# Hybrid decoder block on one core: the prologue's scale sums as columns, and the first token block's work put ahead of the second's

## The chip, the cores and the metric

The kernel runs on one core of a Trainium2 chip. The time is device microseconds (us) of that core for one launch; before the change it is 2329.9 us, the median of three runs (2327.43 to 2331.16). The core has five engines that run side by side, each through its own list of instructions in order: TensorE (PE; the loading of its stationary operand is shown apart as PEld), VectorE (DVE), ScalarE (ACT), GpSimd (POOL) and SyncE (SP), which here only issues DMA transfers. They wait for one another through semaphores.

## The reference, cut to what matters

A decoder block on 2048 tokens of width 1024, with modulation by a vector c, all in float32:

```python
mod = jax.nn.silu(c) @ w_cond[l] + b_cond[l]          # w_cond: 1024 x 6144
shift_m, scale_m, gate_m, shift_f, scale_f, gate_f = [
    m[:, None, :] for m in jnp.split(mod, N_MOD, axis=-1)]

h = rmsnorm(x, g_mix_pre[l]) * (1.0 + scale_m) + shift_m
proj = h @ w_in[l]                                      # w_in: 1024 x 2048
q, k, v, u = jnp.split(proj, [SB_WIDTH, 2 * SB_WIDTH, 3 * SB_WIDTH], axis=-1)
...
x = x + gate_m * rmsnorm(mix, g_mix_post[l])
h = rmsnorm(x, g_ffn_pre[l]) * (1.0 + scale_f) + shift_f
f = (jax.nn.silu(h @ w_gate[l]) * (h @ w_up[l])) @ w_down[l]
x = x + gate_f * rmsnorm(f, g_ffn_post[l])
```

The change lies in the first lines: the sums over c that give the shift and the scale, the norm of the rows, and the first products of `h @ w_in`.

## The kernel before, in words

**Data.** The tokens form four blocks of 512 (`TB`), each of four tiles of 128 rows. The width of 1024 is eight parts of 128 (`kc` or k). `w_in` comes in chunks of 128 output columns, in the order of `chunks`: chunk 0 is q 0, chunk 1 is k 0, chunk 2 is q 1, chunk 3 is u 0, and so on. A float32 operand of a product is held as two f32r tiles, a high one (a cast by ACT, L58) and a low one (source minus high, L59, on DVE or POOL), and a product is three: L68 high by high, L69 with the low half of the tokens, L70 with the low half of the weights (`mm3`). `chunk_split` makes one quarter of a chunk's two tiles: ACT the high, POOL the low.

**Order.** The orders of PE, ACT, DVE and POOL in this phase are those in which the code is written; no scheduler moves anything. SP issues its DMAs in written order too, and a DMA that waits for its buffer holds up all behind it. Chunks' raw weights have two buffers (`w32`); the third chunk's load takes the first chunk's, so it waits for POOL's last low quarter of chunk 0.

**The sums of shift and scale.** silu(c) is `cs`, a column for each kc. The 1024 columns of the shift and those of the scale are done in two halves of 512, half 0 and half 1, and each half in four pairs of kc. `sums_load` issues a pair's two loads of 512 KB (`wcs` for the shift, `wc` for the scale); `sums_step` works on it. The shift is accumulated on DVE as `acc0` (L205 for kc 0, L207 for the others), and needs a sum over the 128 partitions at the end. The scale of half 0 is two products of 1 x 512 a pair on PE (L549, the column of `cs` stationary, the weights moving), which ends as a row. The scale of half 1 is DVE (even kc, L551), ACT (odd kc, L553) and POOL (L555) in `acc1`. `sums_end` turns all into columns: L566 sums `acc0` over the partitions with a moving operand of one column of ones, L572 turns the row into columns (half 0), L570 sums `acc1` (half 1). From these come `am` and `bm`, the multiplier and the addend of the modulation.

**Rows.** The four rows of block 0 (tiles of 128 tokens) are loaded first, squared on ACT for the norm (L297), scaled on DVE, and turned by PE: `turn_rows(j)` makes eight 128x128 transposes of row j (L529) in two banks, copied out by ACT (L533) and DVE (L535) into `turned`. `modulate0` then makes the tokens' high half on ACT (L583), `h` on DVE (L584) and the low half (L585) on POOL for even kc and DVE for odd. Block 1's rows are loaded into `early_lo`, normed, scaled in place (L301: j 0 and 2 on DVE, 1 and 3 on ACT, L301 too), and turned kc by kc (`turn1`, four transposes, L594) behind which the same three steps stand (L583 to L585).

**First products.** `first_products(n, tb, ks)` makes the three products a k for chunk n and block tb. Chunks 0 to 2 are done here for both blocks: k 0 to 3, which need half 0 alone, of block 0 and then of block 1, and then, once half 1 is there, k 4 to 7 of both. The eight banks of PSUM go by name: z0 to z2, w0 and w1 (`t_ps`), a0 and a1, mm. At each finished chunk a store of q or k (cast, low, DMA: `store_qk`) or the pooling sums of u (`pool_ops`, L366 to L388) are queued, one step of which `run_small` emits.

**The rest of the sums.** `rest_of_cond` is a chain of small steps for the parts 2 to 5 of `w_cond` (two gates, the FFN's shift and scale): each step issues one load of 512 KB and one accumulation, on DVE (L205, L207) for kc 0 to 5 and on ACT and POOL for 6 and 7; then come the adding of both (L264), and on PE the gate product `gp` (L236, L237) or the columns `cp` (L218). Six of its steps are emitted among block 1's k 4 to 7. From chunk 3 on, `weave` goes through `pieces` (one k of one chunk and block, three products, at a time), and lets a step of `rest` in every 2.9 pieces, from the first on.

Where the times need a fixed point, it is one of PE's work: 168 groups of three products done and eight turns of block 1's rows.

## Time and profile before

| | |
|---|---|
| runs | 2327.43, 2329.9, 2331.16 us (median 2329.9) |
| profiled execution | 2330.08 us, of which its span (first to last instruction) 2328.3 |
| PE busy | 2260.6 us, 97% of the span |
| PEld busy | 1854.3 us, 80% |
| DVE busy | 1629.2 us, 70% |
| POOL busy | 1317.6 us, 57% |
| ACT busy | 1163.5 us, 50% |
| DMA | 274.51 MB read, 128.45 MB written, mean 174 GB/s |
| granted TensorE clock, mean | 0.990 of full speed |

Shares are of the whole span, of which the part that the change touches is less than a tenth. Times within the span count from the first instruction. A row of the list of instructions in order of time reads: start, duration, engine, line, operation, tiles written <- read, shape, count, and in brackets the idle time ahead and what ended it. A matmul's record ends when its result is out, and records overlap; so the step from one start to the next, not the duration, is what a product takes of PE.

### The profile page before, as it was taken

What the parts mean: (1) busy time and instruction counts of PE and PEld (TensorE: products, weight loads), DVE (VectorE), ACT (ScalarE), POOL (GpSimd) and SP (SyncE); (2) the same over time, 40 slices, a digit from 0 to 9 for tenths busy, and PEclk for the clock granted to TensorE, in tenths of its full rate; (3) what the DMA queues carried; (4) which work ended last, traced back from release to release, by engine and by line L of the source; (5) the groups of instructions that cost most, each with busy time, mean ns of one, the idle gap of its engine ahead of it and who ended that gap; (6) DMA issues with size and microseconds to landing.
All of it is one profiled execution on the core that took longest, in us unless ns stands there. A gap on an engine that the chain in (4) does not pass through costs nothing.

```text
span 2328.3 us, 33054 instructions
## 1 busy us (share of the span) xinstructions
PE 2260.6 (97%) x10589; PEld 1854.3 (80%) x10589; DVE 1629.2 (70%) x2222; ACT 1163.5 (50%) x2411; POOL 1317.6 (57%) x1619
## 2 busy tenths in 40 slices
PE   6999999999999999999999999999999999999997
PEld 4778778888888777887888888888888888888885
DVE  6764549999999966756666565887766556565556
ACT  4323649899999854444323232554533323234444
POOL 4541337787778954555787878331476665641004
PEclk9999999999999999999999999999999999999998
DMA  8785764343435536655545555876754333328554
GB/s 286 257 288 193 259 210 119 99 111 91 128 105 164 161 111 195 213 193 181 171 154 163 158 159 181 272 247 214 257 172 128 99 113 91 114 91 285 189 195 145
DMA packets 307115, 405.15 MB, mean 174 GB/s; under 512 B 19254, under 2 KB 179578, under 8 KB 303868
## 3 DMA queue, kind: packets, MB, share of 16 engines
q1 hardware_dynamic: 302620, 400.68, 53.7%
q10 hardware_dynamic: 4320, 2.36, 0.4%
q8 instruction: 83, 1.36, 0.2%
q14 instruction: 92, 0.75, 0.1%
HBM read 274.51 MB, written 128.45 MB: 173 GB/s over the span
## 4 chain that ended last, share of the span: by engine, by line
PE 81%; DVE 6%; DMA 4%; POOL 4%; issue 3%; ACT 2%; SPq 0%; POOLq 0%; DVEq 0%; ACTq 0%
PE wt L828 4%; PE t_u L70 3%; PE t_u L68 3%; PE t_u L69 3%; PE t_g L69 3%; PE t_g L68 3%; PE t_g L70 3%; PE dn0p L69 3%; PE dn0p L70 3%; PE dn0p L68 3%; PE dn1p L69 3%; PE dn1p L68 3%; PE dn1p L70 3%; PE av L843 3%; PE av L844 2%
## 5 line engine op out<-in xcount | busy, mean ns | idle before, releaser
L817 POOL TENSOR_TENSOR w<-sg,pr 128x512 f32<-128x512 f32 (+2 forms) x320 | 307.3, 960 | 39.8 <-DVE pr L811 21.6
L1177 POOL TENSOR_TENSOR s<-s,cu 128x512 f32<-128x512 f32 x88 | 132.5, 1512 | 238.2 <-DVE cu L1176 145.8
L811 DVE TENSOR_TENSOR_SCAN pr<-pr,carry,begin 128x512 f32<-128x512 f32 x192 | 244.4, 1273 | 0.0
L798 ACT ACTIVATE sg<-z 128x512 f32<-128x512 f32 (+2 forms) x320 | 182.0, 569 | 49.6 <-PE z L796 35.5
L59 DVE TENSOR_TENSOR wtl<-wt,wth 128x512 fp32r<-128x512 f32 (+1 forms) x320 | 189.8, 593 | 20.5 <-ACT wth L58 19.6
L58 ACT CAST wth<-wt 128x512 fp32r<-128x512 f32 (+1 forms) x320 | 181.3, 567 | 13.0 <-PE wt L828 13.0
L800 ACT ACTIVATE pr<-z 128x512 f32<-128x512 f32 (+2 forms) x320 | 181.4, 567 | 0.0
L828 PE MATMUL wt<-ident,w 128*128 128x128 f32 x1088 | 173.9, 274 | 4.7 <-POOL w L817 2.3
L59 DVE TENSOR_TENSOR u_s_l<-u_s,u_s_h 128x512 fp32r<-128x512 f32 x66 | 65.4, 991 | 150.6 <-ACT u_s_h L58 150.6
L828 PEld LDWEIGHTS wt<-ident,w 128*128 128x128 f32 x1088 | 134.8, 141 | 35.4 <-POOL pr L808 3.2
L1167 ACT ACTIVATE s<-s 128x512 f32<-128x512 f32 x88 | 55.7, 633 | 192.0 <-DVE s L1166 192.0
L843 PE MATMUL av<-wth,vt 128*128 128x512 f32 (+1 forms) x320 | 129.9, 406 | 6.4 <-ACT o L848 6.3
L69 PE MATMUL dn0p<-w0p_l,g0p_h 128*128 128x512 f32 x308 | 121.0, 393 | 0.4 <-DVE w0p_l L59 0.4
L68 PE MATMUL dn0p<-w0p_h,g0p_h 128*128 128x512 f32 x308 | 120.6, 392 | 0.0
L70 PE MATMUL dn0p<-w0p_h,g0p_l 128*128 128x512 f32 x308 | 120.5, 391 | 0.0
L59 DVE TENSOR_TENSOR u_a_l<-u,u_a_h 128x512 fp32r<-128x512 f32 x66 | 76.2, 1156 | 62.7 <-ACT u_a_h L58 62.7
L844 PE MATMUL av<-wtl,vt 128*128 128x512 f32 (+1 forms) x320 | 118.5, 370 | 1.5 <-DVE wtl L59 1.3
L795 PE MATMUL z<-kt,qt 128*128 128x512 f32 (+2 forms) x320 | 117.6, 368 | 1.7 <-ACT pr L800 1.5
L58 ACT CAST g_s_h<-g_s 128x512 fp32r<-128x512 f32 x66 | 39.5, 620 | 157.6 <-POOL g_s L1109 80.7
L796 PE MATMUL z<-kt,qt 128*128 128x512 f32 (+2 forms) x320 | 117.1, 366 | 0.0
L69 PE MATMUL dn1p<-w1p_l,g1p_h 128*128 128x512 f32 x292 | 114.5, 392 | 0.0
L68 PE MATMUL dn1p<-w1p_h,g1p_h 128*128 128x512 f32 x292 | 114.3, 392 | 0.0
(652 smaller groups left out, 7184.5 us busy)
## 6 DMA issues: line engine op xcount, KB each, us to landing
g<-in_w_gate_dram SPq DMA_DIRECT2D x42, 512.0 KB, 5.0
u<-in_w_up_dram SPq DMA_DIRECT2D x42, 512.0 KB, 5.2
wc<-in_w_cond_dram SPq DMA_DIRECT2D x32, 512.0 KB, 5.7
qt<-qd SPq DMA_DIRECT2D x64, 256.0 KB, 3.9
wd<-in_w_down_dram SPq DMA_DIRECT2D x44, 256.0 KB, 2.9
tdt<-wd SPq DMA_DIRECT2D x44, 256.0 KB, 2.0
w0p<-tdt SPq DMA_DIRECT2D x44, 256.0 KB, 3.9
w1p<-tdt SPq DMA_DIRECT2D x44, 256.0 KB, 2.9
```

The lines of the kernel that those rows point to most:

```text
L58: nc.scalar.copy(hi, src)
L59: low.tensor_tensor(lo, src, raw(hi), ALU.subtract)
L68: nc.tensor.matmul(ps, lh, rh, start=first and i == 0, stop=False)
L69: nc.tensor.matmul(ps, lh, rl, start=False, stop=False)
L70: nc.tensor.matmul(ps, ll, rh, start=False, stop=last and i == n - 1)
L798: nc.scalar.activation(sg[:, 0:L], z[:, 0:L], AF.Sigmoid, scale=0.125)
L800: nc.scalar.activation(pr[:, 0:L], z[:, 0:L], AF.Sigmoid, scale=-0.125)
L811: nc.vector.tensor_tensor_scan(pr[:, 0:L][:, ::-1], pr[:, 0:L][:, ::-1], begin[:, TB - L:][:, ::-1], zero if carry is None else carry, ALU ...
L817: nc.gpsimd.tensor_tensor(w[:, 0:L], sg[:, 0:L], pr[:, 1:L + 1], ALU.mult)
L828: nc.tensor.transpose(wt[:, i * P:(i + 1) * P], wss[u][i][:, b * P:(b + 1) * P], ident)
L843: nc.tensor.matmul(av[:, lo0:], vb, wh[:, lo0:], start=first, stop=False)
L844: nc.tensor.matmul(av[:, lo0:], vb, wl[:, lo0:], start=False, stop=last)
```

## The change

1. **Scale sums as columns, in both halves.** A pair's scale is now eight products with a 128x128 slice of the weights as the stationary operand and the column of `cs` as the moving one, 128 x 1 each, summed into four columns of a bank (`sums[half]`). The four products that sum `acc0` for the shift go into the same bank. The row, its copy and its turn into columns are gone, and half 1's steps on DVE, ACT and POOL with `acc1` too.
2. **Turns of block 0.** Rows 0, 1 and 2 are turned ahead of the first pair's products, row 3 behind them.
3. **Order of the work.** Block 0 comes whole, chunks 0 to 2 and chunk 3 as well, ahead of block 1. Block 1's turns 0 and 1 stand among chunk 3's products, the others among its own, a pair of k ahead. Chunk 3's block 1 becomes the first piece of the weave.
4. **Loads.** Block 1's four rows are loaded behind all the sums of half 1, the fourth chunk right after, and the fifth chunk's load and splits stand in the prologue and at the start of the weave.
5. **Engines.** One low quarter of chunk 0 and one of chunk 1 go to DVE; all four rows of block 1 are scaled by DVE; their squares go into `junk` instead of a tile of their own.
6. **The rest of the sums.** Eight of its steps instead of six stand ahead of the weave, the others start one piece later, and the steps for v's weights at 96 instead of 104 (the weave has one task less).

The diff, cut to its core:

```diff
-            return lambda: nc.scalar.mul(xs, xt, r) if j % 2 else nc.vector.tensor_scalar_mul(xs, xt, r)
+            return lambda: nc.vector.tensor_scalar_mul(xs, xt, r)
...
-            if not half:
-                nc.tensor.matmul(sums[0:1, :], cs[:, kc:kc + 1], wc[:, kk], start=kc == 0, stop=kc == KC - 1)
-            elif not kk:
-                cond_step(acc1[:, 0], kc, wc[:, kk])
-            else:
-                nc.scalar.mul(wc[:, kk] if pair else acc1[:, 1], wc[:, kk], cs[:, kc:kc + 1])
-                if pair:
-                    nc.gpsimd.tensor_tensor(acc1[:, 1], acc1[:, 1], wc[:, kk], ALU.add)
+            for col in range(4):
+                nc.tensor.matmul(sums[half][:, col:col + 1], wc[:, kk, col * P:(col + 1) * P], cs[:, kc:kc + 1],
+                                 start=kc == col == 0, stop=False)
...
+        for col in range(4):
+            nc.tensor.matmul(ps[:, KC + col:KC + col + 1], acc0[:, (4 * half + col) * P:(4 * half + col + 1) * P], ones[:, 0:1],
+                             start=False, stop=col == 3)
...
-    for pair in range(4):
-        turn_rows(pair)
+    for j in range(3):
+        turn_rows(j)
+    sums_step(0, 0, *coming[0])
+    turn_rows(3)
+    for pair in range(1, 4):
         sums_step(0, pair, *coming[pair])
...
+    chunk_split(loaded[0], 1, nc.vector)
+    sums_end(0)
+    sums[1] = psum("z0", 1, "am1")
+    modulate0(0, 1)
+    first_products(0, 0, 0, 1)
+    chunk_split(loaded[1], 0, nc.vector)
+    chunk_split(loaded[0], 2)
+    modulate0(2, 3)
+    chunk_split(loaded[1], 1)
+    chunk_split(loaded[0], 3)
     loaded.append(chunk_load(chunks[2], 0, [tokp.tile([P, KC, P], F32R, tag="xs", name=f"third{n}") for n in "hl"]))
     coming += [sums_load(1, pair) for pair in range(2, 4)]
...
+    early1 = [row_load(1, j) for j in range(4)]
...
+    sums_end(1)
...
+    pairs = ((0, 1), (2, 3), (4, 5), (6, 7))
+    for ks in pairs[2:]:
         for n in range(3):
             first_products(n, 0, *ks)
+            run_small()
+    for ks in pairs:
+        first_products(3, 0, *ks)
+        if ks[0] < 4:
+            turn1(ks[0] // 2)
+    run_small()
+    for ks in pairs:
+        for n in range(3):
+            first_products(n, 1, *ks)
+            if n < 2 and ks[0] < 6:
+                turn1(ks[0] + 2 + n)
+            run_small()
             if n < 2:
...
+                next(rest)
+            if (n, ks[0]) == (0, 6):
+                loaded.append(chunk_load(chunks[4], 0))
...
     weave(pieces(0, chunks, tasks, loaded),
-          [(rest, 0, 2.9), (v_weight_ops(), 104, 1.9)])
+          [(fifth_ops(), 0, 1), (rest, 1, 2.9), (v_weight_ops(), 96, 1.9)])
```

How this moves instructions, at three places; a row is line, operation, tile written <- tiles read, shape, and how often it stands there in a row.

PE, from the first turn to the first product of chunk 0, before (`x_j_pt` are the turned parts of row j, `wc_0_p` is pair p of the scale's weights in half 0, `acc` the shift's sums):

```order
L549 MATMUL am<-wc_0_0_315,cs 1x512 x2
L529 MATMUL x_1_pt_342<-ident,early_hi 128x128 x4
L529 MATMUL x_1_pt_348<-ident,early_hi 128x128 x4
L549 MATMUL am<-wc_0_1_318,cs 1x512 x2
L529 MATMUL x_2_pt_358<-ident,early_hi 128x128 x4
L529 MATMUL x_2_pt_364<-ident,early_hi 128x128 x4
L549 MATMUL am<-wc_0_2_321,cs 1x512 x2
L529 MATMUL x_3_pt_374<-ident,early_hi 128x128 x4
L529 MATMUL x_3_pt_380<-ident,early_hi 128x128 x4
L549 MATMUL am<-wc_0_3_324,cs 1x512 x2
L566 MATMUL am_columns_424<-ones,acc_310 128x1 x4
L572 MATMUL am_columns_424<-ones,am_row 128x1 x4
```

and of the change, from the turn of row 2 on:

```order
L528 MATMUL x_2_pt_348<-ident,early_hi 128x128 x4
L528 MATMUL x_2_pt_354<-ident,early_hi 128x128 x4
L548 MATMUL am_311<-cs,wc_0_0_313 128x1 x8
L528 MATMUL x_3_pt_370<-ident,early_hi 128x128 x4
L528 MATMUL x_3_pt_376<-ident,early_hi 128x128 x4
L548 MATMUL am_311<-cs,wc_0_1_316 128x1 x8
L548 MATMUL am_311<-cs,wc_0_2_319 128x1 x8
L548 MATMUL am_311<-cs,wc_0_3_322 128x1 x8
L556 MATMUL am_311<-ones,acc_310 128x1 x4
L68 MATMUL first_0_446<-hth_270,wq_0_h 128x512
```

The 512-wide products between the turns are gone; eight one-column products stand in the place of two wide ones, and three such groups follow one another.

SP, the loads behind the first two chunks, before (`early_lo` are block 1's rows, `wcs` and `wc_1_p` the pairs of half 1, the second `wq` the third chunk, `wu` the fourth):

```order
L513 DMA early_lo<-in_x_dram 128x1024 x4
L539 DMA wcs<-in_w_cond_dram 128x2x512
L541 DMA wc_1_0_403<-in_w_cond_dram 128x2x512
...
L413 DMA wq_0_32_410<-in_w_in_dram 128x8x128
L539 DMA wcs<-in_w_cond_dram 128x2x512
L541 DMA wc_1_2_413<-in_w_cond_dram 128x2x512
L539 DMA wcs<-in_w_cond_dram 128x2x512
L541 DMA wc_1_3_416<-in_w_cond_dram 128x2x512
L413 DMA wu_0_32_669<-in_w_in_dram 128x8x128
```

and of the change:

```order
L414 DMA wq_0_32_471<-in_w_in_dram 128x8x128
L538 DMA wcs<-in_w_cond_dram 128x2x512
L540 DMA wc_1_2_474<-in_w_cond_dram 128x2x512
L538 DMA wcs<-in_w_cond_dram 128x2x512
L540 DMA wc_1_3_477<-in_w_cond_dram 128x2x512
L514 DMA early_lo<-in_x_dram 128x1024 x4
L414 DMA wu_0_32_539<-in_w_in_dram 128x8x128
```

The rows have moved from the front to behind the last pair; the third chunk's load still stands ahead of the pairs 2 and 3.

DVE, where block 1's k 4 to 7 are modulated, before (`h_k` is part k of block 1's tokens before its low half is taken off, `acc` from here on the sums of part 2, `q_0` and `k_0` stores):

```order
L584 TENSOR_SCALAR h_4_682<-x_4_677,am,bm 128x512
L584 TENSOR_SCALAR h_5_697<-x_5_692,am,bm 128x512
L585 TENSOR_TENSOR ht1b<-h_5_697,ht1b 128x512
L584 TENSOR_SCALAR h_6_718<-x_6_713,am,bm 128x512
L59 TENSOR_TENSOR q_0_722<-first_0_448,q_0_722 128x512
L584 TENSOR_SCALAR h_7_737<-x_7_732,am,bm 128x512
L585 TENSOR_TENSOR ht1b<-h_7_737,ht1b 128x512
L59 TENSOR_TENSOR k_0_741<-first_0_495,k_0_741 128x512
L59 TENSOR_TENSOR q_0_751<-first_0_553,q_0_751 128x512
L205 TENSOR_SCALAR acc_762<-wc_0_765,cs 128x1024
L258 TENSOR_TENSOR acc_762<-acc_762,br_763 1x1024
```

and of the change, from k 2 on (`us`, `um` and `uf` are the pooling sums of chunk 3's block 0):

```order
L569 TENSOR_SCALAR h_2_741<-x_2_736,am,bm 128x512
L373 TENSOR_TENSOR us_0_1_745<-u_0_725 128x527
L205 TENSOR_SCALAR acc_747<-wc_0_750,cs 128x1024
L258 TENSOR_TENSOR acc_747<-acc_747,br_748 1x1024
L569 TENSOR_SCALAR h_3_766<-x_3_761,am,bm 128x512
L570 TENSOR_TENSOR ht1a<-h_3_766,ht1a 128x512
L384 SCALAR_TENSOR_TENSOR um_0_770<-us_0_1_745,u_0_725 128x512
L387 TENSOR_TENSOR uf_772<-us_0_1_745,rcnt 128x2
L388 TENSOR_TENSOR um_0_770<-uf_772,u_0_725 128x2
L207 SCALAR_TENSOR_TENSOR acc_747<-wc_1_776,cs,acc_747 128x1024
L569 TENSOR_SCALAR h_4_797<-x_4_792,am,bm 128x512
```

Before, all of block 1's modulation stood ahead of the first sum of part 2; now these sums and the pooling stand between its parts.

More of the change, by code (lines that the diff above doesn't have):

```diff
@@ L519, in block_kernel @@
     acc0 = new_acc(0)
-    sums = z_ps("am")
-    row = cond.tile([1, TB], F32, tag="brow", bufs=1, name="am_row")
-    acc1 = cond.tile([P, 2, TB], F32, tag="acc", bufs=2, name="acc1")
+    sums = {0: z_ps("am0")}
     halves = [slice(half * TB, (half + 1) * TB) for half in range(2)]
@@ L597, in block_kernel @@
     first_ps = {}
[L598 removed]
+    first_banks = {(0, 0): mm_only, (3, 0): mm_ps, (0, 1): av_ps, (1, 1): av_ps}
     def first_products(n, tb, *ks):
@@ new lines, in block_kernel, with fifth_ops @@
+    for ks in pairs:
[9 more added lines that the diff above has]
+            run_small()
+            if n < 2:
+                next(rest)
+            if (n, ks[0]) == (0, 6):
+                loaded.append(chunk_load(chunks[4], 0))
+    def fifth_ops():
+        for part in range(4):
+            chunk_split(loaded[4], part)
+            yield
@@ L679, in block_kernel @@
+    tasks = [(n, tb) for n in range(3, len(chunks)) for tb in range(2)][1:]
     wvs = []
```

95 lines of the change are left out of this document (29 added, 66 removed).

## The prediction

> **What bounds the kernel now.** I read the page first, then stretches of the prologue, then TensorE's waits, then its instructions in order of time. The stretches:
>
> ```profile
> 0.00:82.20 82.20, 62.09 (x257) 43.61 (x258) 54.95 (x83) 37.17 (x66) 36.10 (x61) 0.92 0.77 265
> 100.00:110.00 10.00, 5.72 (x24) 3.84 (x22) 9.93 (x10) 5.41 (x9) 6.82 (x5) 0.98 0.79 281
> 160.00:200.00 40.00, 40.00 (x178) 33.13 (x177) 24.03 (x40) 13.59 (x35) 11.28 (x15) 1.00 0.65 213
> ```
>
> The columns are stretch, length, busy time of PE, PEld, DVE, ACT and POOL, granted clock, DMA share, GB/s. PE is the bound: in 160 to 200 us it is busy throughout, in the first 82 only for 62. What it loses before 170 us moves the end. After the gate product of part 5 (near 170 us) each engine's order is the same in both kernels, so the change is worth what it does to PE's time before that, one for one.
>
> ```profile
> PE am_columns L566 <- DVE acc L207: 3.7, 2, 3.1
> PE u L68 <- DVE k L59: 2.5, 1, 2.5
> PE cp L218 <- DVE acc L264: 1.3, 1, 1.3
> PE gp L236 <- ACT gs2xt L58: 1.0, 1, 1.0
> PE gp L237 <- DVE gs2xs L59: 0.8, 1, 0.8
> PE k L70 <- POOL wk_l L59: 1.2, 1, 1.2
> ```
>
> Most of the first (3.1) is the wait for the half-1 sums, which now have fewer steps on DVE; the other five (6.8 us) come after 100 us, where DVE is late with the remaining sums (the stretch above has it at 9.93 of 10 us) and POOL once with a split. My fixed mark is the moment when PE has done 168 products of three-term groups (chunks 0 to 2 for both blocks, chunk 3 for the first) and eight turns of a chunk of the second block's rows: before, that is where chunk 3 begins the second block, 87.64.
>
> ```profile
> 82.20 0.39 PE L68 MATMUL u<-hth,fourthh 128*128 128x512 f32 x1
> 87.64 0.39 PE L68 MATMUL u<-ht1a,fourthh 128*128 128x512 f32 x1
> ```
>
> 24 products in 5.44 us: 0.227 us each at full clock, 38.1 us for 168.
>
> **Part 1, the scale sums of half 0.**
>
> ```profile
> 8.88 1.97 PE L529 MATMUL x_pt<-ident,early_hi 128*128 128x128 f32 x8 [4.71 <-DVE x_v L111]
> 12.86 3.57 PE L549 MATMUL am<-wc,cs 128*1 128x512 f32 x4 [2.01 <-DMA wc<-in_w_cond_dram]
> 17.93 1.88 PE L549 MATMUL am<-wc,cs 128*1 128x512 f32 x4
> 19.74 1.09 PE L529 MATMUL x_pt<-ident,early_hi 128*128 128x128 f32 x8
> 26.09 1.02 PE L566 MATMUL am_columns<-ones,acc 128*128 128x1 f32 x8 [0.62 <-DVE acc L207]
> 27.04 1.24 PE L572 MATMUL am_columns<-ones,am_row 1*128 1x1 f32 x8
> 29.64 0.79 PE L68 MATMUL first<-hth,wq_h 128*128 128x512 f32 x1 [1.37 <-ACT hth L583]
> 30.99 0.79 PE L69 MATMUL first<-htl,wq_h 128*128 128x512 f32 x1 [0.56 <-POOL htl L585]
> 123.91 1.92 PE L218 MATMUL cp<-ones,acc 128*128 128x1 f32 x16 [1.34 <-DVE acc L264]
> 143.09 1.84 PE L218 MATMUL cp<-ones,acc 128*128 128x1 f32 x16
> ```
>
> A pair's row sum takes 1.88 us. The new form is eight column products with a 128x128 f32 stationary, which the trace has as L218: 16 records, 1.84 to 1.92. So a pair costs the same on PE at full clock; L572's 1.24 goes, and half 1, which used no PE for its scale sums, gains 4 x 1.9 = 7.6 us.
>
> The clock makes the difference. The same view cut finer around the columns, with PE's busy time, clock, DMA share and GB/s, then single records:
>
> ```profile
> 26.09:27.74 1.65, 1.65 (x15) 1.00 1.02 405
> 27.74:28.30 0.56, 0.54 (x4) 0.52 1.00 402
> 127.50:129.00 1.50, 1.50 (x5) 0.50 0.33 131
> 27.51 0.56 PE L572 MATMUL am_columns<-ones,am_row 1*128 1x1 f32 x3
> 27.73 0.55 PE L572 MATMUL am_columns<-ones,am_row 1*128 1x1 f32 x2
> 27.93 0.35 PE L572 MATMUL am_columns<-ones,am_row 1*128 1x1 f32 x1
> ```
>
> The clock is halved at 27.74, in the middle of a burst of one-column products, 1.65 us of "busy" after the last wide product; and again at 127 us, after the burst at 123.91. Where it falls, the step between records goes from 0.11 (27.51 to 27.73, two records) to 0.20. So I take it that such bursts do not hold the clock up, and cost 16 x 0.20 = 3.2 us when it is down. Before, it was the 512-wide row sums at 12.86 (3.57 us at half speed, then 1.88) that raised it. In the changed half 0 PE has only turns and bursts until the first product. The Trainium skill, "TensorE: Matmul & The Clock Gate", Part 4, says that transposes do not count as busy towards the full clock. By that rule the trace agrees: the turns at 8.88 take 1.97 us and the row sums behind them still start at half speed. The Trainium skill, same page, Part 1, says that the clock falls after an idle window of about 3.4 us; if a burst is not idle, that gives the second rival.
>
> ```profile
> 13.18 0.69 DVE L535 COPY turned<-x_pt 128x512 f32<-128x512 f32 x1
> ```
>
> Row 1's turn needs the bank that this copy frees, near 13.8, since the copies stand behind the four scalings on DVE. Then, at half clock: turns 1 and 2, 2 x 1.9 = 3.8 (17.6); burst 3.2 (20.8); turn 3, 1.8 (22.6); three bursts 9.6 (32.2); four columns of the shift sums 1.8: **34.0**, where before they end at 28.28. With 1.36 from there to the first product: 35.4 against 29.64, **+5.7**. DVE's sums, which let the columns start at 26.09 before, hide behind it. At full clock the same chain ends at 27.1: -1.2, the other bound.
>
> **Part 2, from the first product to the mark.** Before: 87.64 - 29.64 = 58.0. After, by terms: products 38.1; eight turns of a chunk's rows at half of what a row's turn takes at 19.74 (0.45 from start to start), 3.6; half-1 bursts 7.6 and four columns 1.0; the 1.36 again behind the second sums; two waits for a low half as at 30.99, 0.9 each, 1.8; 11 products at half clock at the start, 2.2, and 9 behind the second sums, 1.9; the last half-1 bursts at half clock, because only 6 products (1.4 us) stand between them, 2.5 (bounds 0 and 5); and what the second block waits for.
>
> ```profile
> 66.87 0.81 DVE L584 TENSOR_SCALAR h<-x,am,bm 128x512 f32<-128x512 f32 x1 [1.87 <-ACT ht1b L583]
> 77.48 1.03 DVE L205 TENSOR_SCALAR acc<-wc,cs 128x1024 f32<-128x1024 f32 x1
> 78.55 1.21 DVE L258 TENSOR_TENSOR acc<-acc,br 1x1024 f32<-1x1024 f32 x1
> 86.87 1.28 DVE L207 SCALAR_TENSOR_TENSOR acc<-wc,cs,acc 128x1024 f32<-128x1024 f32 x1
> 69.47 0.69 DVE L585 TENSOR_TENSOR ht1b<-h,ht1b 128x512 fp32r<-128x512 f32 x1
> 91.75 0.71 DVE L372 TENSOR_TENSOR us<-u 128x527 f32<-128x527 f32 x1 [0.77 <-POOL u L366]
> 92.50 1.27 DVE L383 SCALAR_TENSOR_TENSOR um<-us,u 128x512 f32<-128x512 f32 x1
> 93.69 0.69 DVE L386 TENSOR_TENSOR uf<-us,rcnt 128x2 f32<-128x2 f32 x1
> ```
>
> Now a turn stands one pair of chunks ahead of its use, with DVE's sums of parts 2 between. Between turn 2's and turn 3's h stand a pooling sum (0.71), 1.03 and 1.21. They begin about when turn 3 ends on PE, and h (0.81) and the low half (0.69) follow: 4.45 us, against the ten products, 2.3 us, that PE has before it needs that half: 2.1 late. In the next pair 1.27, 0.69, a correction of the same kind and 1.28 are ahead of h 4, and 1.28 ahead of h 5; the same count gives 1.35 and 0.65, and 0.45 in the last pair, where one sum stands ahead of each. Together 4.5 (bounds 0 and 7). Sum: 38.1 + 3.6 + 8.6 + 1.4 + 1.8 + 2.2 + 1.9 + 2.5 + 4.5 = 64.6, **+6.6**. The mark moves to 100.0, **+12.3**.
>
> **Moved at no cost.** All four rows are now scaled by DVE, two of them by ACT before:
>
> ```profile
> 36.66 1.57 DVE L301 TENSOR_SCALAR early_lo<-early_lo,x_r 128x1024 f32<-128x1024 f32 x2
> ```
>
> 0.79 more for each of two, and the rows' loads come last; both lie beside the 36 products of k 4 to 7 and the first of chunk 3 (some 10 us after the second sums). By the landing below, the rows are there at about 56 us, before those products begin; only a landing after 65 would cost. The two low halves given to DVE (some 0.6 each) take the place of POOL's and lie beside the half-clock products. The fourth chunk's splits lie beside the same 10 us; the fifth chunk's now start with the second block of chunk 3, 5.4 us of products, with one 128x1024 add ahead of them on POOL: cost nothing, up to 1.
>
> **What half 1 waits for besides.**
>
> ```profile
> 24.67 3.22 POOL L59 TENSOR_TENSOR wq_l<-wq,wq_h 128x256 fp32r<-128x256 f32 x4 [12.19 <-ACT wq_h L58]
> 27.91 0.37 SPq L413 DMA_DIRECT2D wq<-in_w_in_dram  x1
> 6.07 1.06 ACT L297 ACTIVATE xt<-early_hi 128x1024 f32<-128x1024 f32 x1 [3.50 <-DMA early_hi<-in_x_dram]
> ```
>
> SP issues the third chunk's load when POOL has the fourth low of chunk 0 (27.89); the last two pairs of sums and all four rows are behind it in SP's queue. Before, POOL does those lows in a row; now two low halves of the tokens and one low of chunk 1 stand between. From the first product on these are twice 1.35 (as from 29.64 to 30.99), three times 0.8, and some 1.4 for DVE's next h: near 42 us. DMA is then idle from about 30; a first load landed some 3 us after its issue (the first row, issued at 2.7, let this ACT row begin), and each further 512 KB takes 1.3 at the 400 GB/s above: third 45, last pair 51, rows 56. PE comes to the last pair at about 51 as well (35.4, the 1.35, 11 half-clock products 4.7, three bursts 5.7, 18 products 4.1). Cost nothing, up to 4.
>
> **Part 3, after the mark.** The same order of next sums, about two steps later against PE. Their four loads' slots come free by DVE steps that are now finished earlier against PE, and k's store stands one DVE sum earlier, so the waits of 2.5 + 1.3 + 1.0 + 0.8 can go, and with them the half clock behind two of them (one is the row at 127.50; some 3.4 us each, half of it lost, 3.4 together); POOL's 1.2 too, since its add now stands behind those lows. In all 10.2. But the stretch from 100 us has DMA at 0.79, and the loads that DVE waited for still pass through it, so I count six tenths, **-6.1** (bounds 0 and -10.2).
>
> **Sum.** +12.3 - 6.1 = +6.2 on the profiled execution's 2330.08 us (0.2 above the median of 2329.9): **2336**.
>
> **Rivals.** *All of the later waits go* (0.20): -10.2 instead of -6.1, 2332. For it: nearly all are DVE's lateness. Against: new ones follow where DMA is this busy. *Not slower, the clock holds through turns and bursts* (0.15): half 0 at -1.2 instead of +5.7, 2.5 less in half 1, in all 9.4 less: 2326.5. It decides at 17.6 us: if the first burst takes 1.9, this is it. For it: the burst at 143.09, among products, was followed by full clock. Against: 27.74. *The third load holds half 1 up* (0.20): 4 us more for the last pair, and 1.5 more on DVE: 2341.5. For it: DMA would idle from about 30 to 42 us. My forecast has 0.45, and 2332 to 2341 of its own.
>
> **How the numbers follow.** Within 0.2% (which a measurement here can about tell from no change) is 2325.2 to 2334.6. Forecast: 0.31 slower, 0.14 same; all waits gone: same; clock holds: 0.09 faster, 0.06 same; third load: slower. Faster 0.09, same 0.40, slower 0.51. The range, 2325 to 2343, takes in all but the tails of the outer two.
>
> **What would show it.** A first product near 35 us and bursts of 3.2 us in half 0; the mark near 100; DVE as releaser of L69 in the second block, 4 to 5 us in all; fewer waits of gp, cp and u. Wrong, if the first product comes before 31 us, or if PE is clocked down little between 14 and 60 us.

## The result, and the profile after

The changed kernel takes 2336.36 us, the median of eight runs (2331.27 to 2339.05); the kernel before takes 2326.9, the median of eight. The ratio is 1.0037, with an interval of 1.0024 to 1.005: 8.6 us slower (5.6 to 11.6). The ratio is that of the means; the medians are 9.5 us apart. The profiled execution took 2338.89 us, with a span of 2337.1; that of before 2330.08. The predicted 2336 is met, but 3 us of that are owed to the base: the first three runs of before, on which it was built, have a median of 2329.9, all eight one of 2326.9. Against its own base the prediction said +6.2.

The stretches of the prologue in the changed kernel (columns as before: busy PE, PEld, DVE, ACT, POOL, clock, DMA share, GB/s):

```profile
0.00:82.20 82.20, 65.46 (x305) 56.80 (x306) 41.81 (x71) 28.64 (x54) 26.79 (x56) 0.79 0.70 241
100.00:110.00 10.00, 10.00 (x46) 8.28 (x45) 5.09 (x7) 5.86 (x11) 5.40 (x4) 1.00 0.90 321
```

In the first 82 us PE is now busier than before (65.5 of them, 62.1 before), at a mean clock of 0.79 instead of 0.92. (This column reads 1.00 until the clock first falls in a trace, also where it is still down: it has 1.00 for 0 to 18.2 us, where the eight turns at 9.30, shown below, take 1.97 us instead of 1.07. So ahead of the first fall the speed is read from the records.) In 100 to 110, where PE waited and DVE was full, it is the other way round.

Three points of PE's work are the same in both kernels: the first product of chunk 0, the mark, and the first turn of the pooling weights (L708 before, L706 now), behind which nothing is moved. The mark is 168 single products, 56 groups of three (the section on the kernel before calls them 168 groups), and eight turns of block 1's rows. Between the mark and that turn PE has the same number of instructions in every kernel below (463 to 465 in these views, by what their edges cut). The stretches between these points, first before, then after:

```profile
29.64:87.64 58.00, 50.42 (x216) 40.05 (x217) 45.88 (x58) 29.47 (x51) 32.82 (x29) 0.90 0.70 233
87.64:201.22 113.58, 106.22 (x464) 86.29 (x463) 74.13 (x95) 32.94 (x72) 49.99 (x51) 0.97 0.78 259
201.22:2328.30 2127.08, 2086.91 (x9846) 1719.89 (x9844) 1494.73 (x2040) 1090.14 (x2268) 1227.95 (x1506) 0.99 0.52 166
```

```profile
33.20:102.72 69.52, 63.19 (x272) 50.97 (x273) 43.53 (x59) 24.53 (x45) 27.90 (x27) 0.81 0.65 219
102.72:209.16 106.44, 104.14 (x464) 85.27 (x463) 76.06 (x92) 34.41 (x75) 52.87 (x50) 0.98 0.79 263
209.16:2337.10 2127.94, 2085.45 (x9846) 1716.85 (x9844) 1499.04 (x2040) 1090.46 (x2268) 1225.94 (x1506) 0.99 0.52 166
```

The first product comes 3.6 us later (33.20 for 29.64), the stretch to the mark is 11.5 longer, the next is 7.1 shorter, the last 0.9 longer: 8.8 in all. What the clock takes from a stretch is at most its length times one minus the clock: to the mark 5.8 us before, 13.2 after (11.7, if only PE's busy time at half clock counts); behind it 3.4 and 2.1. The prediction took the gate product of part 5 (gp, near 170 us) for the end of what is moved. What stands behind it is indeed the same, but it stands nine products later in the changed kernel, so the turn of the pooling weights is the better point.

Of PE's waits in the changed kernel:

```profile
PE first L69 <- DVE ht1a L570: 2.3, 1, 2.3
PE u L68 <- DVE q L59: 1.5, 1, 1.5
PE am L548 <- DMA wc<-in_w_cond_dram: 0.8, 1, 0.8
PE u L68 <- DVE k L59: 0.6, 1, 0.6
PE cp L218 <- DVE acc L264: 0.2, 1, 0.2
```

The 3.1 us for half 1's sums are gone, and so are the waits of gp and of k for `wk_l`; those of cp and u are down from 4.3 to 2.3 us. New are 2.3 for DVE's low half of k 3 and 0.8 for a pair of half 1.

Half 0 on PE, in order of time:

```profile
9.30 1.97 PE L528 MATMUL x_pt<-ident,early_hi 128*128 128x128 f32 x8 [5.13 <-DVE x_v L111]
14.34 3.87 PE L528 MATMUL x_pt<-ident,early_hi 128*128 128x128 f32 x16 [3.07 <-DVE turned L534]
18.00 1.98 PE L548 MATMUL am<-cs,wc 128*128 128x1 f32 x16
19.84 1.07 PE L528 MATMUL x_pt<-ident,early_hi 128*128 128x128 f32 x8
20.74 9.39 PE L548 MATMUL am<-cs,wc 128*128 128x1 f32 x48
29.99 1.84 PE L556 MATMUL am<-ones,acc 128*128 128x1 f32 x8
33.20 0.80 PE L68 MATMUL first<-hth,wq_h 128*128 128x512 f32 x1 [1.37 <-ACT hth L568]
```

Row 1's turn waits for the bank until 14.34, as predicted (13.8). Then comes what was not predicted: the first burst takes 1.98 us, full speed, and turn 3 1.07. Only the three bursts in a row are slow, 9.39 us. The clock in finer stretches:

```profile
18.30:21.60 3.30, 3.30 (x32) 3.30 (x32) 2.02 (x4) 1.11 (x2) 0.00 (x0) 1.00 1.09 359
21.70:38.70 17.00, 15.08 (x59) 13.62 (x60) 10.92 (x18) 4.85 (x10) 5.28 (x5) 0.50 0.51 163
38.80:48.90 10.10, 9.29 (x62) 8.06 (x61) 5.36 (x6) 1.94 (x6) 5.54 (x8) 1.00 0.78 267
49.00:66.00 17.00, 15.02 (x51) 12.78 (x51) 7.90 (x16) 7.36 (x13) 5.38 (x7) 0.50 0.66 242
```

It is up from 18.3, though PE had done nothing but turns from 14.34 to 18.0. It falls at 21.7, behind a window with one burst, one turn and the start of the next bursts, and falls again at 49, in half 1, behind the wait of 0.8 for a load and a burst. Each stretch at half clock is 17 us long, and 15 us of it are busy.

### The profile page after: what moved, and what is told of

Read it like the earlier page. It is cut to its first block, busy times and chain, and to the rows that moved or that the text cites. A ratio compares the mean times of both kernels' runs of the same rounds, so it can differ in the third digit from the quotient of the medians.

```text
span 2337.1 us, 33225 instructions
## 1 busy us (share of the span) xinstructions
PE 2272.6 (97%) x10685; PEld 1871.9 (80%) x10685; DVE 1633.7 (70%) x2221; ACT 1159.3 (50%) x2404; POOL 1311.0 (56%) x1614
## 4 chain that ended last, share of the span: by engine, by line
PE 80%; DVE 6%; DMA 4%; POOL 4%; issue 3%; ACT 3%; SPq 0%; POOLq 0%; DVEq 0%; ACTq 0%
PE wt L826 4%; PE t_g L69 3%; PE t_g L68 3%; PE t_g L70 3%; PE t_u L70 3%; PE t_u L69 3%; PE t_u L68 3%; PE dn0p L69 3%; PE dn0p L68 3%; PE dn0p L70 3%; PE dn1p L69 3%; PE dn1p L68 3%; PE dn1p L70 3%; PE av L841 2%; PE av L842 2%
## 5 line engine op out<-in xcount | busy, mean ns | idle before, releaser
L815 POOL TENSOR_TENSOR w<-sg,pr 128x512 f32<-128x512 f32 (+2 forms) x320 | 307.3, 960 | 38.8 <-DVE pr L809 23.0
```

The lines of the kernel that those rows point to most:

```text
L815: nc.gpsimd.tensor_tensor(w[:, 0:L], sg[:, 0:L], pr[:, 1:L + 1], ALU.mult)
```

## The experiments

Two theories to begin with. **Clock theory** (the prediction's): most of the cost is that bursts of one-column products let the clock fall, in half 0 and in half 1. **Order theory**: the cost is that block 1's products no longer cover half 1's sums and loads; the clock is a by-product. Every ratio below is to the kernel before, run on the same chip, with its 95% interval; the times of the three points are from one profiled execution each.

| kernel | first product | mark | turn of pooling weights | ratio |
|---|---|---|---|---|
| before | 29.64 | 87.64 | 201.2 | 1 |
| changed | 33.20 | 102.72 | 209.2 | 1.0037 (1.0024 to 1.005) |
| rows_half0 | 30.27 | 94.88 | 205.9 | 1.0012 (1.0003 to 1.002) |
| rows_both | 29.81 | 95.89 | 205.3 | 1.0023 (1.0014 to 1.0033) |
| order_alone | 29.13 | 98.00 | 207.1 | 1.0031 (1.0019 to 1.0043) |
| columns_alone | 34.71 | 93.20 | 208.1 | 1.0027 (1.0018 to 1.0035) |
| pairs_first | 36.78 | 101.48 | 208.7 | 1.0044 (1.0028 to 1.0061) |
| sums_later | 36.92 | 99.28 | 217.4 | 1.0065 (1.0053 to 1.0077) |
| more_turns | 31.79 | 101.54 | 213.4 | 1.0019 (1.001 to 1.0029) |
| cover | 29.83 | 98.06 | 208.1 | 1.005 (1.0036 to 1.0064) |
| columns_half1 | 30.22 | 87.39 | 200.2 | 0.9997 (0.9988 to 1.0006) |
| columns_half1_rest_early | 30.10 | 87.42 | 203.7 | 1.0019 (1.001 to 1.0027) |
| columns_half1_store_late | 28.86 | 84.68 | 197.1 | 0.9999 (0.999 to 1.0007) |
| columns_half1_filled | 27.36 | 84.56 | 197.9 | 1.0001 (0.9993 to 1.001) |

### Undoing the columns, or doing them alone

**rows_half0**, on the changed kernel:

```diff
+            if not half:
+                nc.tensor.matmul(sums[half][0:1, :], cs[:, kc:kc + 1], wc[:, kk], start=kc == 0, stop=kc == KC - 1)
+                continue
             for col in range(4):
...
```

The rest of the edit, in `sums_end`, puts back the copy of half 0's row and its four turns into columns.

> The changed kernel, with the scale sums of half 0 alone put back to 512-wide row products (a copy and four 1x1 turns of the row with them). Clock theory (one-column bursts let the clock fall, and that is most of the cost): the first product comes at about 30 us instead of 33.2, the first long stretch at half clock (21.67 to 38.74 in the changed kernel) shrinks to 7 us or less, half 1 stays as it is: some 4 us less than the changed kernel, ratio to before 1.002. Order theory (the cost is that block 1's products no longer cover half 1's sums and loads, the clock is a by-product): the gain ahead of half 1 is lost in the wait for it; within 1 us of the changed kernel, 1.0037.

Measured: 1.0012, 5.8 us less than the changed kernel; first product at 30.27. Its stretches:

```profile
19.10:29.20 10.10, 9.66 (x40) 3.82 (x38) 6.28 (x12) 1.87 (x4) 1.00 (x1) 1.00 1.10 352
29.30:36.00 6.70, 5.18 (x11) 3.76 (x12) 6.01 (x9) 4.14 (x8) 4.80 (x4) 0.50 0.26 95
```

The stretch at half clock is 6.8 us, as the clock theory said (7 or less), and begins only when PE waits for the first tokens. The same busy time on PE, as wide products, keeps the clock.

**rows_both**, on the changed kernel:

```diff
-            for col in range(4):
-                nc.tensor.matmul(sums[half][:, col:col + 1], wc[:, kk, col * P:(col + 1) * P], cs[:, kc:kc + 1],
-                                 start=kc == col == 0, stop=False)
+            nc.tensor.matmul(sums[half][0:1, :], cs[:, kc:kc + 1], wc[:, kk], start=kc == 0, stop=kc == KC - 1)
...
```

The copy and the turns of the row come back in `sums_end` for both halves.

> The changed kernel, with the scale sums of both halves as 512-wide row products; TensorE's own work for a pair is the same (1.9 us), and each half gains a copy and a turn of the row (some 2 us in its chain). Clock theory: the second stretch at half clock (48.98 to 66.05) shrinks as well: 3 us of half-clock bursts and some 5 us of half-clock products less than the changed kernel beside the 4 us of half 0, 2 us more for the row: 8 to 10 us less in all, ratio 0.999 to 1.0005. Order theory: the same or 2 us more than the changed kernel, 1.0037 to 1.0045.

Measured: 1.0023, not less than rows_half0, and far from the 0.999 to 1.0005 expected. The expectation took the second stretch at half clock (49 to 66) for the doing of half 1's bursts. In rows_half0, with the same bursts, that stretch is 6.8 us already (49.7 to 56.5), so the bursts of half 1 do not make its length. What rows in half 1 add is their copy and their turn; the stretch to the mark is 66.1 us (64.6 in rows_half0).

**order_alone**, on the changed kernel:

```diff
+            if not half:
+                nc.tensor.matmul(sums[half][0:1, :], cs[:, kc:kc + 1], wc[:, kk], start=kc == 0, stop=kc == KC - 1)
+            elif not kk:
+                cond_step(acc1[:, 0], kc, wc[:, kk])
+            else:
+                nc.scalar.mul(wc[:, kk] if pair else acc1[:, 1], wc[:, kk], cs[:, kc:kc + 1])
+                if pair:
+                    nc.gpsimd.tensor_tensor(acc1[:, 1], acc1[:, 1], wc[:, kk], ALU.add)
...
```

`sums_end` goes back with it to the form of before.

> The changed kernel's order and loads with the sums of before: row products in half 0, VectorE, ScalarE and GpSimd in half 1. Clock theory: no burst but the columns of the two ends; TensorE waits for half 1's sums some 8 us (to about 54 us, first product of part 4 at about 55.5 instead of 59.5), with the clock down behind that wait: 5 us less than the changed kernel, ratio 1.0015. Order theory: the order itself costs what the change costs, 1.003 or more.

Measured: 1.0031, the order theory's number. PE's waits:

```profile
PE am_columns L573 <- DVE acc L207: 3.7, 1, 3.7
PE first L68 <- ACT thirdh L58: 2.9, 1, 2.9
PE am_columns L576 <- DVE acc L570: 0.6, 1, 0.6
```

With half 1's sums on DVE, and nothing of block 1 to do meanwhile, the wait for them is 4.3 us, beside 2.9 for the third chunk's cast, and the clock falls behind them. So the new order needs half 1 as columns: they are worth 4.4 us there (1.0031 to 1.0012; the two intervals just touch).

**columns_alone**, on the kernel before: the `for col` loop of the change in its `sums_step` for both halves.

> The kernel before, in its own order, with the scale sums of both halves as columns. Clock theory: with turns and bursts alternating the clock is down from 13 us or a little later until products stand close, the first product comes at 33 to 35 us instead of 29.6, and half 1's 7.6 us of bursts take the place of 3.1 us of waiting: 7 to 10 us more than before, ratio 1.003 to 1.004. Order theory: only TensorE's own work counts, 7.6 - 3.1 - 1.2 = 3.3 us more, ratio 1.0015 or less.

Measured: 1.0027; first product at 34.71, as the clock theory had it.

```profile
13.03 3.57 PE L547 MATMUL am<-cs,wc 128*128 128x1 f32 x16 [1.79 <-DMA wc<-in_w_cond_dram]
16.46 1.95 PE L527 MATMUL x_pt<-ident,early_hi 128*128 128x128 f32 x8
18.20 3.41 PE L547 MATMUL am<-cs,wc 128*128 128x1 f32 x16
```

Turn by turn and burst by burst, each runs at half speed until the first product (by these records; the clock column has no fall yet there and reads 1.00). The stretch to the mark is then 58.5 us (58.0 before): half 1's columns cost nothing in the old order.

**columns_half1**, on the kernel before: the same for half 1 alone, rows in half 0.

> The kernel before, in its own order, with half 1's scale sums alone as columns (half 0 keeps its row products). Clock theory: single bursts among products do not let the clock fall, the 3.1 us of waiting for VectorE go, the first product stays at 29.6: what is added and what is saved are alike, ratio 0.9995 to 1.001. Theory that TensorE's added work is the price: 7.6 - 3.1 = 4.5 us more, ratio 1.002.

Measured: 0.9997, the clock theory's number, and no gain over before that can be measured. So half 0's columns cost 7.0 us in the old order (1.0027 to 0.9997) and 5.8 in the new one; the order, its loads and its engines, with half 1 as columns, cost 3.5 (1.0012 to 0.9997). Each theory has a part of the cost. The steps from before to columns_half1, rows_half0 and the changed kernel, -0.7 + 3.5 + 5.8, make up the 8.6 by their nature, so this is a division and not a check; each step is known to some 3 us, by the intervals of its ends. The traces of these two show where the order costs, rows_half0 first:

```profile
30.27:94.88 64.61, 59.09 (x272) 47.89 (x273) 43.83 (x59) 24.47 (x45) 27.88 (x27) 0.85 0.70 232
```

```profile
30.22:87.39 57.17, 54.53 (x273) 45.16 (x273) 39.98 (x53) 27.01 (x47) 27.73 (x26) 0.92 0.71 235
```

The same instructions of PE in both; in the new order it idles 2.9 us more (64.61 - 59.09 against 57.17 - 54.53), behind half 1's sums (1.4) and for the low halves of k 3 (2.3) and k 6 (0.7), less 1.5 for the third chunk, and loses up to 9.7 us to the clock instead of 4.6. Both executions stand at different ends of their spreads, so of these 7 us only 3.5 are in the medians.

### The step that was wrong: do turns hold the clock up?

**more_turns**, on the changed kernel:

```diff
+    more = psum("a0", 1, "more_turns")
     for j in range(3):
         turn_rows(j)
+        for k in range(0 if j else 14):
+            nc.tensor.transpose(more[:, k % 4 * P:(k % 4 + 1) * P], ready[0][:, k % 8 * P:(k % 8 + 1) * P], ident)
```

> The changed kernel, with 14 more turns of row 0 into a spare bank, which nobody reads, between the turns of rows 0 and 1, where TensorE waits 3.1 to 3.6 us for that row's copy anyway. If turns hold the clock up as products do, the clock rises at 14 to 17.5 us in every execution instead of at 18.3 in some and at 40 in others, turns 1 and 2 and the first burst run at full clock, and the three bursts after turn 3 let it fall again: the first product at 31 to 33 us, 1 to 3 us less than the changed kernel, ratio 1.0025 to 1.0033, by adding work. If turns do not count, as the prediction took it, the first product stays at 36.8 whenever the clock was down, and the time is that of the changed kernel or up to 1 us more, 1.0037 or more.

Measured: 1.0019, some 4 us less than the changed kernel, where 1 to 3 were expected, by adding work (the two intervals overlap by a twentieth of a per cent). First product at 31.79, inside the 31 to 33 expected if turns count:

```profile
11.00 2.96 PE L599 MATMUL more_turns<-ident,early_hi 128*128 128x128 f32 x14
14.42 1.09 PE L528 MATMUL x_pt<-ident,early_hi 128*128 128x128 f32 x8 [0.46 <-DVE turned L534]
15.86 1.09 PE L528 MATMUL x_pt<-ident,early_hi 128*128 128x128 f32 x8 [0.35 <-DVE turned L534]
16.79 1.84 PE L548 MATMUL am<-cs,wc 128*128 128x1 f32 x16
18.49 1.07 PE L528 MATMUL x_pt<-ident,early_hi 128*128 128x128 f32 x8
19.40 9.31 PE L548 MATMUL am<-cs,wc 128*128 128x1 f32 x48
```

Turn 1 is at full speed at 14.42 (1.09 us), with only turns before it. order_alone shows the same without an added turn, its row sums at full speed right behind turns 1 and 2 and nothing wider before:

```profile
14.00 3.47 PE L529 MATMUL x_pt<-ident,early_hi 128*128 128x128 f32 x16 [3.06 <-DVE turned L535]
17.40 1.88 PE L549 MATMUL am<-wc,cs 128*1 128x512 f32 x4
```

So turns count, and the bursts behind them do not. The trace of more_turns does not show where the 4 us of the medians lie: it is the slowest of the eleven executions (2340.51 us), and behind the mark, where the clock is 0.94 (0.98 in the changed kernel), it loses more than the earlier first product gave.

Compare half 0 of **sums_later** (below), whose instructions up to there are word for word those of the changed kernel:

```profile
14.94 3.86 PE L528 MATMUL x_pt<-ident,early_hi 128*128 128x128 f32 x16 [3.61 <-DVE turned L534]
18.60 3.41 PE L548 MATMUL am<-cs,wc 128*128 128x1 f32 x16
23.61 10.24 PE L548 MATMUL am<-cs,wc 128*128 128x1 f32 x48
36.92 0.80 PE L68 MATMUL first<-hth,wq_h 128*128 128x512 f32 x1 [1.36 <-ACT hth L568]
```

The two turns begin 0.6 us later, and here they do not raise the clock: the first product is at 36.92. In the changed kernel's trace the clock's steps lie at 18.3, 21.7, 38.7, 49.0 and 66.1: distances of 3.41 us, or three or five times that. So the clock goes by windows of that length. Turns of 3.7 us fill such a window, or they straddle two of them and fill neither. The traces bear this out: in the changed kernel the turns fill 92% of the window that ends at 18.3; in sums_later the clock first falls at 57.66, and counted back from there in steps of 3.41 a window ends at 16.7, in the middle of the turns, so that they fill about half of it and half of the next. In pairs_first (below) they fill 80% of a window, counted back in the same way, and the clock stays down; in order_alone 86% raise it.

### The other suspects

**pairs_first**, on the changed kernel:

```diff
-    coming = [sums_load(1, pair) for pair in range(2)]
+    coming = [sums_load(1, pair) for pair in range(4)]
...
-    coming += [sums_load(1, pair) for pair in range(2, 4)]
```

> The changed kernel, with the last two pairs of half 1's sums issued by SP right behind the first two, ahead of the third chunk's load, so that they don't wait for GpSimd's fourth low part at 40.0 us. Third-load rival: the last pairs are on chip long before TensorE comes to them, the wait of 0.81 goes and with it most of the half clock behind it; part 4 begins at 54 to 56 us instead of 59.5, 3 to 5 us less than the changed kernel, ratio 1.0015 to 1.0025. Clock theory without it: half 1 is bound by TensorE's own bursts, 1 us less at most, 1.0033 or more.

Measured: 1.0044, not faster. The third load does not hold half 1 up by more than the 0.8 us of the wait. In its trace the stretch to the mark is 64.7 us, but with the old loads that of sums_later is 62.4, so the loads are not what shortened it; both have less half clock there, some 15 and 14 us against 26 in the changed kernel.

**sums_later**, on the changed kernel (by this edit the first four of the eight steps go one pair of k later and the last four by one or two chunks' products, less than the expectation says):

```diff
-            if n < 2:
+            if ks[0] >= 2 and (n < 2 or ks[0] >= 4):
                 next(rest)
```

> The changed kernel, with the eight steps of the remaining sums moved two pairs of k later (none ahead of the second pair, two more behind the third chunk's products in the last two pairs), so that VectorE has none of them between turns 2 and 5 of block 1. The prediction's step on VectorE: the wait of 2.28 us and the half clock behind it (86.53 to 89.94, 1.6 us) shrink to less than 1 together, and up to 2 us come back after the mark where the sums are later: 1 to 3 us less than the changed kernel, ratio 1.0025 to 1.0033. If the wait is for block 1's rows or for ScalarE instead, it stays, 1.0037 or more.

Measured: 1.0065, 6.5 us more instead of 1 to 3 less. The wait of 2.28 for k 3 did go (1.6 are left, for another k), but behind the mark the stretch is 118.1 us instead of 106.4:

```profile
PE u L68 <- DVE q L59: 3.4, 1, 3.4
PE k L70 <- POOL wk_l L59: 3.2, 1, 3.2
PE k L68 <- ACT wk_h L58: 2.2, 1, 2.2
```

The fifth chunk's splits come late: ACT's begin 7.4 us after the mark (106.67), 3.8 in the changed kernel (106.51). Ahead of them on ACT stand the second step of L252 and a cast of q that waits 5.4 us for an earlier store of q to land (2.7 in the changed kernel). POOL's step L255 stands ahead of its low quarters. So where the sums stand changes what is lost behind the mark. But the waits for gp and cp, 3.1 us before, do not come back here (0.4), so the earlier start of the sums is not what removed those; what did stays open.

**columns_half1_rest_early**, on columns_half1:

```diff
     rest = rest_of_cond()
+    for _ in range(2):
+        next(rest)
```

> As columns_half1, and two more steps of the remaining sums ahead of block 1's second half (eight in all ahead of the weave, as in the changed kernel). If VectorE's lateness after the mark is what the 7.4 us of waits there come from, 2 to 4 us less than columns_half1, ratio 0.998 to 0.9995: faster than both kernels. If the loads behind the stores in SP's queue set the pace, no gain: the same as columns_half1.

Measured: 1.0019, slower, against both expectations. The two steps also put gp 4 us earlier into PE's list, and there PE waits for what DVE and ACT cannot give sooner: 5.0 us at gp (2.1 in columns_half1) and 3.4 at u (1.0).

**columns_half1_store_late**, on columns_half1:

```diff
-            nc.sync.dma_start(mtd[tb][4 + g], m)
+            if n_late == 0:
+                nc.sync.dma_start(mtd[tb][4 + g], m)
+        n_late = 5 if tb < 2 else 0
         yield mean
+        if n_late:
+            for _ in range(n_late):
+                yield lambda: None
+            yield lambda: nc.sync.dma_start(mtd[tb][4 + g], m)
```

> As columns_half1 (0.9997), with the store of the pooled sums five small steps later, so that the loads of the remaining sums are ahead of it in SP's queue: before, SP stood at the store until VectorE had finished the sums it stores (94.4 us), and VectorE then waited 2 to 5.5 us at a time for those loads. If VectorE's lateness after the mark comes from that, its waits for these loads shrink from 16 us to a third, as in the changed kernel, TensorE's 5.5 us of waits for gp, cp and u mostly go, and the half clock behind them: 2 to 5 us less than columns_half1, ratio 0.9977 to 0.999, faster than both kernels. If the loads are late for want of bandwidth (DMA is at 0.8 to 0.9 there), no gain.

Measured: 0.9999, no gain. PE's waits behind the mark stay at 6.0 us (5.5 in columns_half1). DVE's waits for these loads (76 to 175 us) went from 16.2 us to 12.9, not to a third. So SP's place at the store is not what makes DVE late, or not alone; whether the bandwidth is, this run does not show. (What the section on the kernel before says of SP, written order, holds for the loads of the prologue; further on its list departs from it, as where two loads into `spare` stand ahead of stores of q that are written before them.)

**cover**, on rows_half0:

```diff
+    chunk_split(loaded[3], 0)
+    chunk_split(loaded[3], 1)
     sums_end(1)
+    first_products(3, 0, 0, 1, 2, 3)
...
-    chunk_split(loaded[3], 0)
-    chunk_split(loaded[3], 1)
...
-    for ks in pairs:
+    for ks in pairs[2:]:
+        turn1(ks[0] // 2 - 2)
         first_products(3, 0, *ks)
-        if ks[0] < 4:
-            turn1(ks[0] // 2)
```

> As rows_half0 (1.0012), and chunk 3's k 0 to 3 of block 0 right behind the columns of half 1, where TensorE waited 1.43 and 0.55 us for the modulation of k 4; chunk 3's first two splits stand ahead of half 1's end for it, and the turns 0 and 1 ahead of its k 4 to 7. If the order's own cost is the cover that block 1's products gave half 1's sums before, these waits go and the half clock behind them (49.75 to 56.58 in rows_half0) shrinks: 2 to 4 us less than rows_half0, ratio 0.9995 to 1.0004. If it comes from VectorE's steps between block 1's turns, the same as rows_half0.

Measured: 1.005, 9 us more than rows_half0 instead of 2 to 4 less. The wait that was to be covered came back in another dress:

```profile
PE first L68 <- ACT fourthh L58: 3.6, 1, 3.6
```

The fourth chunk's load lands only at 52.4, and its cast now stands ahead of the modulation on ACT. The theory behind it, that the lost cover is the order's cost, is neither shown nor refuted by this kernel.

**columns_half1_filled**, on columns_half1:

```diff
+    def more_turns(n):
+        for k in range(n):
+            nc.tensor.transpose(more[:, k % 4 * P:(k % 4 + 1) * P], ident, ident)
...
         turn_rows(pair)
+        if not pair:
+            more_turns(8)
         sums_step(0, pair, *coming[pair])
+    more_turns(6)
...
     sums_end(0)
+    more_turns(12)
```

> As columns_half1 (0.9997), with turns of the identity into a spare bank, which nobody reads, in half 0's waits: 8 behind row 0's turn, 6 ahead of the columns of the shift, 12 behind those of the scale, where TensorE waits 1.4 us for the modulated tokens. If the share of a window of some 3.4 us that wide products and turns fill is what holds the clock, the half clock around the first products (28.82 to 35.65 in columns_half1) shrinks by one window or both: 1 to 3 us less than columns_half1, ratio 0.9984 to 0.9993, faster than both kernels. If the fall there has another cause, no gain, and up to 0.5 us more for turns that outlast a wait: 0.9997 to 0.9999.

Measured: 1.0001, no gain in time. The clock did what was expected, and more:

```profile
12.40:43.00 30.60, 26.48 (x143) 16.48 (x141) 19.94 (x34) 16.11 (x30) 14.02 (x17) 1.00 1.07 370
```

It is up from 12.4 to 43 (by the records: the row sums at 13.05 take 1.88 us, full speed), the first product comes at 27.36, the mark at 84.56, 2.8 us ahead of columns_half1. At the turn of the pooling weights 2.3 us of that are left in the traces, and nothing is in the medians. The profiled execution of the filled kernel is the fastest of its twelve (2323.14 us; seven lie above 2326.8), that of columns_half1 the third of eleven, so these traces show lucky executions; where the gain goes in the others is open. No kernel tried is faster than the one before.

## Why the prediction was right, and where it was not

**The sign and the size** were right: slower, by 8.6 us (5.6 to 11.6) where +6.2 was said. The likeliest case, that half 0's columns let the clock fall, is shown by rows_half0 from one side and columns_alone from the other. That the total came so near is partly luck: in the profiled execution half 0 cost 2.1 us less than said, the stretch to the mark 4.9 more, the one behind it gave back 1.0 more and the rest of the program added 0.9; and the base had moved by 3.

**Half 0, +5.7.** Measured in the profiled execution: +3.6, and 36.8 to 36.9 for the first product, +7.2, in two kernels with the same half 0. The three bursts in a row took 9.39 us (9.6 said). What failed is the step "In the changed half 0 PE has only turns and bursts until the first product", which took turns for idle. The Trainium skill, "TensorE: Matmul & The Clock Gate", Part 4, says that transposes do not count as busy towards the full clock; here these float32 turns do, as the 1.09 us of turn 1 in more_turns shows, and the measurement decides. The row that the prediction read in favour of that rule, row sums at half speed behind 1.97 us of turns, showed only that 1.97 us, with 2.01 of waiting behind them, are too short. The Trainium skill, same page, Part 1, says that the window, about 3.4 us long, runs freely of the kernel; the distances of 3.41 us between the clock's steps, and first products at 33.2 and 36.9 from the same instructions, agree with it.

**To the mark, +6.6.** Measured: +11.5. The term that was mis-sized is the clock: 2.2, 1.9 and 2.5, in all 6.6 us, were counted, and 11.7 to 13.2 were lost (up to 5.8 before): the two long stretches, with products in them, stayed down for 17 us each. The other terms nearly held. The 72 one-column records cost 10.9 us, counted from each group's start to the next start in the list (11.1 said for bursts and columns with their half clock); the waits were 6.3 (7.7 said), among them the one at k 3:

```profile
83.72 1.21 DVE L258 TENSOR_TENSOR acc<-acc,br 1x1024 f32<-1x1024 f32 x1
84.86 0.79 DVE L569 TENSOR_SCALAR h<-x,am,bm 128x512 f32<-128x512 f32 x1
85.69 0.69 DVE L570 TENSOR_TENSOR ht1a<-h,ht1a 128x512 fp32r<-128x512 f32 x1
86.43 0.73 PE L69 MATMUL first<-ht1a,wq_h 128*128 128x512 f32 x1 [2.28 <-DVE ht1a L570]
```

2.28 us, 2.1 said, by the steps named. The further three (1.35, 0.65, 0.45) did not come but for 0.67 at k 6, on POOL; so DVE holds PE up by 2.3 us there, where 4 to 5 were said.

**Behind the mark, -6.1.** Measured: -7.1, of which 5.1 are waits (7.4 to 2.3 us) and up to 1.3 the clock. That the place of the sums against PE's work bears on it is shown by sums_later, where the stretch is 11.7 us longer; but gp and cp stay without waits there, so what removed these is open. That the relief can be had without the later mark is not shown: both attempts in the old order failed. A reading that fits, but is not shown, is that PE comes 15 us later and finds DVE's sums done.

**The rivals.** That all later waits go (-10.2) did not hold: 5.1 of 7.4 us went, and -7.1 is nearer to the -6.1. That the clock holds fell, and so did its test: the first burst did take 1.9 us, and the clock still fell one window later, at 21.7. That the third load holds half 1 up fell with pairs_first, though SP did stand at it until 40.0 (42 said). The cost of the new order by itself, 3.5 us, stood in no rival; the prediction had it spread over its waits. Which part of the order, its loads or its engines makes it stays open: cover and sums_later were to show it, and both came out slower for other waits.

## What to carry to other kernels

Two ways of using TensorE with the same busy time need not be alike: a product with one moving column is busy in the profile, but a run of them lets the clock fall, and the half clock lasted 17 us in the changed kernel, with wide products in it. So price such an edit with the clock that comes after it, and try whether a few turns in a wait that exists anyway hold it up (here that gave some 4 us in one kernel and nothing that can be measured in another). And where an order gives waits back late in the program, ask whether it saves time or only arrives later.

## What the runs showed of the hardware

Turns raise the clock like wide products: 3.7 us of them did so when they filled 92% of a window, and two windows filled by about half did not. Bursts of the changed kernel in half 1:

```profile
39.10 1.84 PE L548 MATMUL am<-cs,wc 128*128 128x1 f32 x16
43.67 1.84 PE L548 MATMUL am<-cs,wc 128*128 128x1 f32 x16
47.84 2.56 PE L548 MATMUL am<-cs,wc 128*128 128x1 f32 x16 [0.81 <-DMA wc<-in_w_cond_dram]
```

The first two stand alone between products, and the clock stays up (the stretch from 38.8 to 48.9 above); the third, behind a wait of 0.8 us, ends at half speed, as three in a row did in half 0. The window's place differs from execution to execution, which is a likely reason, though not a shown one, why one kernel's times spread: the changed kernel over 7.8 us, more_turns over 13.6 (2326.9 to 2340.5), the kernel before over 7.0 in the eight runs beside the changed one. With such spreads one profiled execution fixes a cost of this kind to some 4 us and no better (an estimate, half of the smaller two).
